# Output projection by seven block products, with its gated weights and block sums formed on GpSimd during the attention

## The chip, the cores and the metric

The kernel runs on one core of a Trainium2 chip. The metric is the device time in microseconds of one execution. The engines are called TensorE (PE; PEld is its weight load), VectorE (DVE), ScalarE (ACT), GpSimd (POOL) and SyncE (SP), which issues most of the DMAs.

## The reference, cut to what matters

One transformer layer over 1024 latent tokens of width 1024, with 256 context tokens. Two groups of heads (four retention heads, four heads of differential attention) give 1024 columns side by side; one output projection `w_out` follows, its result is gated by `g1` and added to `x`; then norm, MLP, norm.

```python
y_ret_lat = jax.nn.silu(rg_l) * ret_lat                    # 4 heads x 128 columns
y_diff_lat = diff_subln(diff_attention(dq_l, k_all, v_all, lam), subln_g, lambda_init)   # 4 x 128
out_lat = jnp.concatenate([y_ret_lat, y_diff_lat], axis=-1) @ w_out      # (1024, 1024)
x = x + g1 * out_lat
h = rms_norm(x, norm2_g) * (1.0 + sc2) + sh2               # into the MLP
```

All of it is in float32. A matmul is made in three passes: both operands are split in a high part (`F32R`, rounded) and a low part (the rest), and high x high, high x low and low x high are summed in PSUM (`passes`).

## The kernel before, in words

The stages come one after the other: modulation and input projection, retention (its results go to `yr_d` in DRAM, already split), differential attention, output projection, MLP.

The attention runs over 32 units (`Unit`, four heads times eight tiles of 128 queries). A unit has two score matrices of 128 x 1280 (`scores`, L897), their least values on VectorE (`least`, L900), two exponentials on ScalarE (`exp`, L904), the ratio of the two sums and the combination of the two on VectorE (`ratio`, L908 and L909; `combine`, L912, 128 x 1280 with both operands in SBUF), transposes and the product with the values (L917, L929), and a norm: a copy and a square on ScalarE (L933, L938), `e` on GpSimd (L940), `rstd` with L943 on VectorE and a power on GpSimd (L944), `norm` on ScalarE (L947), a transpose (L952), and the high and low part of the result (L955 on ScalarE, L958 on VectorE). The units overlap; the table `TAU` gives each step its place, and `in_order` fixes this order on PE, DVE, ACT and SP. What stands in `tc.issue_after(units[u].pool_ins.ins)` is issued behind L944 of unit `u`.

The output projection takes each of two column halves of `w_out` and in it eight row tiles of 128 tokens: 8 blocks times 3 passes of 128 x 512 matmuls into one bank, then a multiplication with `g1` and an addition to `x1` on VectorE. The weights of the first half are split in eight units in the middle of the attention, one block a unit: a cast on ScalarE (L1110), the low part on GpSimd (L1111). `yT` holds both parts of all activations in SBUF.

When a row tile of `x1` is complete, `norm2` stores it, squares it on ScalarE and scales it by a power made on GpSimd (L117). The first four rows are turned (`turned0`) beside the second half of the projection, the last four (`turned1`) beside the first products of the MLP. The MLP itself already uses seven block products; its first weights (`pre`, `raws`, in the slots `wra` and `wrb` of the pool `wst`) are loaded around the end of the attention, and `sums_in_place` adds blocks of them on GpSimd.

Of the kernel before, what the change touches and what calls it, by code (L numbers as in the profile page):

```python
# [26 lines left out]
H = 4  # L27
# [33 lines left out]
TAIL = 2  # L61
SPARE = (16, 4)
# [12 lines left out]
def kernel(  # L75
# [39 lines left out]
    def rsqrt(out_ap, in_ap, mul, eps, n):  # L115
        nc.vector.tensor_scalar(out=out_ap, in0=in_ap, scalar1=mul, scalar2=eps, op0=ALU.mult, op1=ALU.add)
        nc.gpsimd.tensor_tensor(out=out_ap, in0=out_ap, in1=mhalf[:, :n], op=ALU.pow)  # L117
# [29 lines left out]
    yr_d = [dr.tile([P, 2, H, 512], F32, name=f"yrd{i}") for i in range(2)]  # L147
# [7 lines left out]
    with ExitStack() as p1:  # L155
# [98 lines left out]
        class Step:  # L254
# [54 lines left out]
            def turn(self):  # L309
                pt = pst.tile([P, P], F32, name="pyt", tag="tr")  # L310
                nc.tensor.transpose(pt, self.y, ident)
                c = self.t % 2 * P
                if c == 0:
                    steps["out"] = rt.tile([P, 2, 2 * P], F32R, name="yr")
# [3 lines left out]
                if c == P:  # L318
                    o = (self.t % 4 - 1) * P
                    nc.sync.dma_start(out=yr_d[self.t // 4][:, :, self.h, o : o + 2 * P], in_=r32(steps["out"]))  # L320
# [562 lines left out]
        class Unit:  # L883
# [18 lines left out]
            def exp(self, m):  # L902
                self.p[m] = al.tile([P, LK], F32, name=f"p{m}")
                nc.scalar.activation(self.p[m], self.pa[m][:, :LK], AF.Exp, scale=-1.0, bias=self.mt[:, m : m + 1], accum_out=self.s[:, m : m + 1])  # L904
# [44 lines left out]
            def final(self):  # L949
                self.hi, self.lo = (yT[a][self.qt // 4][:, H + self.h, self.qt % 4 * P : (self.qt % 4 + 1) * P] for a in range(2))  # L950
# [3 lines left out]
            def high(self):  # L954
                nc.scalar.activation(self.hi, self.py, AF.Copy, scale=self.gain)  # L955

            def low(self):
                nc.vector.scalar_tensor_tensor(out=self.lo, in0=self.py, scalar=self.gain, in1=r32(self.hi), op0=ALU.mult, op1=ALU.subtract)  # L958
# [129 lines left out]
    ctx_ya = ctx.enter_context(ExitStack())  # L1088
    ypa = ctx_ya.enter_context(tc.tile_pool(name="ypa", bufs=1, reuse_waits="tile"))
    ctx_y = ctx.enter_context(ExitStack())  # L1090
    ypb = ctx_y.enter_context(tc.tile_pool(name="ypb", bufs=1, reuse_waits="tile"))
    yT = [[p.tile([P, KD, 512], F32R, name=f"yT{a}{i}") for i, p in enumerate((ypa, ypb))] for a in range(2)]

    ctx_wo = ctx.enter_context(ExitStack())
    wo = ctx_wo.enter_context(tc.tile_pool(name="wo", bufs=1, reuse_waits="tile"))

    g1 = wo.tile([P, D], F32, name="g1")

    def out_weights(n, sl, eng=nc.sync, low=nc.vector, lag=0):
        raws = []  # L1100
        for k in range(KD + lag):
            if k < KD:
                raw = wo.tile([P, 512], F32, name="woraw", bufs=4)
                eng.dma_start(out=raw, in_=w_out[n][:, k, :])
                raws.append(raw)
            yield
            if k >= lag:
                whi = wo.tile([P, 512], F32R, name="wohi", bufs=9)
                wlo = wo.tile([P, 512], F32R, name="wolo", bufs=9)
                nc.scalar.copy(whi, raws[k - lag])  # L1110
                low.tensor_tensor(out=wlo, in0=raws[k - lag], in1=r32(whi), op=ALU.subtract)  # L1111
                sl.append((whi, wlo))

    wo_first = []
    wo_gen = out_weights(0, wo_first, nc.gpsimd, nc.gpsimd, 2)


    with ExitStack() as p2:
        gap = p2.enter_context(tc.tile_pool(name="gap", bufs=1, reuse_waits="tile")).tile([P, 3200], F32, name="gap")
# [5 lines left out]
        for n in range(n_units + 8):  # L1125
# [3 lines left out]
            if n == 9:  # L1129
                with tc.issue_after(units[n - 5].pool_ins.ins):  # L1130
                    nc.gpsimd.dma_start(out=g1, in_=g1_d)
            if n in (8, 10, 12, 14):
                a, i = divmod(n // 2 - 4, 2)
# [705 lines left out]
```

## Time and profile before

| | us |
|---|---|
| median of 3 runs (lowest, highest) | 1388.02 (1388.01, 1388.24) |
| span of the profiled execution, first to last instruction | 1386.3 |
| own time of the profiled execution | not given apart from its span |
| attention, from its steady state to its last score tiles | 489.8 to 640.7 |
| end of the attention, output projection | 640.7 to 743.8 |

The granted TensorE clock was 0.999 in the mean. Positions are microseconds from the start of the span. In the rows of a profile, a line `L912 DVE ... out<-in x9 | 14.0, 1551 | 0.3` is a group of nine instructions of line 912 on VectorE, 14.0 us busy together, 1551 ns each in the mean, with 0.3 us of idle time ahead of them. In a row of the timeline the first two numbers are start and duration in us, and the brackets hold how long the engine had been idle and for whom it waited. Matmuls overlap: their rows show 0.39 us, but the next starts earlier, and the distance of starts counts.

### The profile page before, as it was taken

How to read it: one execution, taken by the hardware profiler on the slowest of the kernel's cores; microseconds unless marked ns; L12 is line 12 of the kernel's file. 1: busy time of each engine (PE TensorE's matmuls, PEld its weight loads, DVE VectorE, ACT ScalarE, POOL GpSimd, SP SyncE). 2: the span in 40 equal slices, each digit the busy share in tenths (PEclk: the TensorE clock that was granted, in tenths of full speed). 3: DMA queues.
4: the chain of work that ended last, by engine and by line, in shares of the span. 5: the costliest groups of instructions: out<-in, count | busy, mean ns of one | idle time of the engine just before them, and what ended most of it. 6: DMA issues, size and time to landing. Idle time of an engine off the chain costs nothing.

```text
span 1386.3 us, 19666 instructions
## 1 busy us (share of the span) xinstructions
PE 1365.4 (98%) x7028; PEld 1145.9 (83%) x7028; DVE 1018.0 (73%) x1512; ACT 738.6 (53%) x1410; POOL 346.4 (25%) x384
## 2 busy tenths in 40 slices
PE   8999999999999999999999999999999999999997
PEld 6788788888888799998888888888888888888886
DVE  5967866623467898896347998887778877898756
ACT  5536534313466789987037654555545555455533
POOL 1310001501446433411101343222332220043003
PEclk9999999999999999999999999999999999999999
DMA  9467887786678488631221223332323326953334
GB/s 384 153 206 252 295 265 249 254 273 185 191 221 231 133 217 186 140 94 70 106 99 46 92 107 114 114 114 92 114 100 113 111 69 224 393 180 109 122 99 152
DMA packets 107305, 231.14 MB, mean 167 GB/s; under 512 B 9604, under 2 KB 42884, under 8 KB 105288
## 3 DMA queue, kind: packets, MB, share of 16 engines
q1 hardware_dynamic: 98936, 204.73, 43.3%
q0 software_dynamic: 8128, 24.91, 7.9%
q8 instruction: 55, 0.90, 0.3%
q14 instruction: 42, 0.34, 0.1%
q10 hardware_dynamic: 144, 0.26, 0.1%
HBM read 165.37 MB, written 64.23 MB: 166 GB/s over the span
## 4 chain that ended last, share of the span: by engine, by line
PE 65%; DVE 1%; POOL 1%; issue 0%; ACT 0%; DMA 0%; SPq 0%; POOLq 0%; ACTq 0%; DVEq 0%
PE chain L131 6%; PE chain L132 6%; PE chain L133 6%; PE c L132 5%; PE c L133 5%; PE c L131 5%; PE pv L929 5%; PE pA L897 5%; PE third L131 3%; PE third L133 3%; PE third L132 3%; PE pt L917 2%; PE po L133 2%; PE po L132 2%; PE po L131 2%; PE second L131 1%
## 5 line engine op out<-in xcount | busy, mean ns | idle before, releaser
L131 PE MATMUL pl<-hT,whi 128*128 128x512 f32 x256 | 107.6, 420 | 0.0
L131 PE MATMUL chain<-T,whi 128*128 128x512 f32 x264 | 102.8, 389 | 0.0
L132 PE MATMUL chain<-T,whi 128*128 128x512 f32 x264 | 102.7, 389 | 0.0
L133 PE MATMUL chain<-T,wlo 128*128 128x512 f32 x264 | 102.7, 389 | 0.0
L133 PE MATMUL pl<-hT,wlo 128*128 128x512 f32 x256 | 100.4, 392 | 0.0
L132 PE MATMUL pl<-hT,whi 128*128 128x512 f32 x256 | 100.3, 392 | 0.0
L900 DVE TENSOR_REDUCE mt<-pA 128x1 f32<-128x1280 f32 x64 | 95.2, 1490 | 3.8 <-PE pA L897 2.3
L133 PE MATMUL c<-whi,ghl 128*128 128x512 f32 x232 | 90.4, 390 | 0.0
L131 PE MATMUL c<-whi,ghl 128*128 128x512 f32 x232 | 90.3, 389 | 0.0
L132 PE MATMUL c<-wlo,ghl 128*128 128x512 f32 x232 | 90.3, 389 | 0.0
L1310 POOL TENSOR_TENSOR cmb<-wrb 128x512 f32<-128x512 f32 x20 | 30.3, 1517 | 237.6 <-DMA wrb<-w_up 157.3
L897 PE MATMUL pA<-ks,qhl 128*128 128x512 f32 (+1 forms) x384 | 89.6, 368 | 0.0
L904 ACT ACTIVATE p<-pA,mt 128x1280 f32<-128x1280 f32 x64 | 85.5, 1336 | 3.8 <-DVE mt L900 3.4
L131 PE MATMUL pn<-whi,hT 128*128 128x512 f32 x192 | 85.0, 443 | 0.0
L445 ACT ACTIVATE xb<-pl 32x512 f32<-32x512 f32 (+1 forms) x88 | 52.0, 591 | 61.6 <-PE pl L133 41.9
L1161 ACT CAST whi<-cmb 128x512 fp32r<-128x512 f32 x62 | 38.4, 622 | 77.5 <-PE chain L132 64.3
L929 PE MATMUL pv<-va,aT 128*128 128x128 f32 x640 | 77.1, 276 | 0.4 <-DVE yT L958 0.3
L897 PEld LDWEIGHTS pA<-ks,qhl 128*128 128x128 f32 x384 | 67.9, 189 | 11.5
L133 PE MATMUL pn<-whi,hT 128*128 128x512 f32 x192 | 75.8, 396 | 1.0 <-POOL hT L610 1.0
L132 PE MATMUL pn<-wlo,hT 128*128 128x512 f32 x192 | 75.4, 393 | 0.0
L929 PEld LDWEIGHTS pv<-va,aT 128*128 128x128 f32 x640 | 74.0, 192 | 1.2 <-DVE yT L958 0.8
L1162 DVE TENSOR_TENSOR wlo<-cmb,whi 128x512 fp32r<-128x512 f32 x62 | 58.7, 951 | 18.1 <-ACT whi L1161 18.1
(336 smaller groups left out, 3889.7 us busy)
## 6 DMA issues: line engine op xcount, KB each, us to landing
raw<-w_in SPq DMA_DIRECT2D x32, 512.0 KB, 6.0
wm<-w_mod SPq DMA_DIRECT2D x32, 512.0 KB, 4.6
wra<-w_up SPq DMA_DIRECT2D x24, 512.0 KB, 3.3
wrb<-w_up SPq DMA_DIRECT2D x23, 512.0 KB, 3.5
W<-w_down SPq DMA_DIRECT2D x44, 256.0 KB, 6.2
ad<-s SPq DMA_DIRECT2D x20, 512.0 KB, 3.4
wra<-ad SPq DMA_DIRECT2D x20, 512.0 KB, 3.3
wrb<-ad SPq DMA_DIRECT2D x18, 512.0 KB, 4.6
```

The source lines that it names most:

```text
L131: mm(ps, lh, rh, start=first, stop=False, skip_group_check=more)
L132: mm(ps, lh, rl, start=False, stop=False, skip_group_check=more)
L133: mm(ps, ll, rh, start=False, stop=last, skip_group_check=more)
L445: nc.scalar.activation(xb[q * blk : (q + 1) * blk, :], pt[o : o + blk, :], AF.Copy, scale=scale)
L897: mm(self.pa[m][:, c0:c1], self.q[:, i, m, qs], self.k[:, m, c0:c1], start=(i == 0), stop=(i == 1))
L900: nc.vector.tensor_reduce(out=self.mt[:, m : m + 1], in_=self.pa[m][:, :LK], axis=AX.X, op=ALU.min)
L904: nc.scalar.activation(self.p[m], self.pa[m][:, :LK], AF.Exp, scale=-1.0, bias=self.mt[:, m : m + 1], accum_out=self.s[:, m : m + 1])
L917: nc.tensor.transpose(self.pt[g][:, i, :], self.p[0][:, (4 * g + i) * P : (4 * g + i + 1) * P], ident)
L929: mm(self.pv, self.aT[:, c, :], self.v[:, c, :], start=(c == 0), stop=(c == NKT - 1))
L1161: nc.scalar.copy(hi, src)
L1162: nc.vector.tensor_tensor(out=lo, in0=src, in1=r32(hi), op=ALU.subtract)
L1310: nc.gpsimd.tensor_tensor(out=s1, in0=b1, in1=b2, op=ALU.add)
```

## The change

The activations Y and the weights W are seen as 2 x 2 blocks (tokens 0 to 511 and 512 to 1023; retention and attention columns; the two halves of the outputs), and the product is made by seven block products with sums of blocks (the variant of Winograd) in place of eight. A block product is four row tiles times four blocks of 128 times three passes, 48 matmuls. Four of the seven products go into one set of four banks (`chain`, `oc`), which is added to `x1` after each of them and never started anew; the others go into a second set (`os`, `of`).

The gate is multiplied into the weights. A generator `weight_blocks` yields GpSimd operations of 128 x 512: the gated blocks with their high and low parts, and the differences t1 to t4, which go to DRAM (`wt_d`) through the SP queue and come back in the projection. It also forms `s3` from the retention results, and a list `later` holds sums that need finished heads of the attention. `next_op` gives one such operation, and three are issued behind L944 (now L953) of each unit from iteration 6 on, until the 76 are used up. The loads of `w_out` and `g1` move from GpSimd's queue to SP's. In a unit L958 (the low part on VectorE) is gone; results stay whole in `y12` and `y22` and are split in the projection, or per head for `opb`.

On GpSimd, in a stretch of the attention, this stood before (L944 is the power, L940 `e`, L1111 a low part of a projection weight, L981 a load of queries):

```order
178 L944 TENSOR_TENSOR ssa<-ssa,mhalf 128x1
179 L940 TENSOR_TENSOR e<-sa 128x1
180 L1111 TENSOR_TENSOR wolo<-woraw,wohi 128x512
181 L944 TENSOR_TENSOR ssa<-ssa,mhalf 128x1
182 L940 TENSOR_TENSOR e<-sa 128x1
183 L981 DMA qhl<-dq_89 64x4x512
184 L1111 TENSOR_TENSOR wolo<-woraw,wohi 128x512
```

and this stands there now (L953 is the power, L949 `e`, L1140 an operation of `weight_blocks`, L1192 one of `later`, L997 the load of queries):

```order
206 L953 TENSOR_TENSOR ssa<-ssa,mhalf 128x1
207 L1140 TENSOR_TENSOR w11o<-w_5629,w11o 128x512
208 L1140 TENSOR_TENSOR w21o<-w_5631,g_5016 128x512
209 L949 TENSOR_TENSOR e<-sa 128x1
210 L997 DMA qhl<-dq_89 64x4x512
211 L1140 TENSOR_TENSOR w_5631<-w_5631,g_5016 128x512
212 L997 DMA qhl<-dq_89 64x4x512
213 L953 TENSOR_TENSOR ssa<-ssa,mhalf 128x1
```

Where one operation of 128 x 512 (or none) stood between two powers, there are three, and the loads of queries, keys and values stand between them.

At the end of the projection GpSimd had this before (L117 is the power for a row tile of `x1`, L1225 to L1227 are `sums_in_place`, L1307 is a sum of the MLP's weights; `x7` stands for seven in a row):

```order
221 L1225 TENSOR_TENSOR wrb<-wrb 128x512
222 L1226 TENSOR_TENSOR wra<-wrb,wra 128x512
223 L1227 TENSOR_TENSOR wra<-wra 128x512
224 L117 TENSOR_TENSOR sm_7022<-sm_7022,mhalf 128x1 x7
225 L1307 TENSOR_TENSOR cmb<-wrb,wra 128x512
```

and has this now (L118, L1299 to L1301, L1455):

```order
276 L118 TENSOR_TENSOR sm_7088<-sm_7088,mhalf 128x1 x4
277 L1299 TENSOR_TENSOR wrb<-wrb 128x512
278 L1300 TENSOR_TENSOR wra<-wrb,wra 128x512
279 L1301 TENSOR_TENSOR wra<-wra 128x512
280 L118 TENSOR_TENSOR sm_7088<-sm_7088,mhalf 128x1 x3
281 L1455 TENSOR_TENSOR cmb<-wrb,wra 128x512
282 L118 TENSOR_TENSOR sm_7088<-sm_7088,mhalf 128x1
```

The sums stood ahead of all but one of these powers; now four powers come first, and the powers of the last four rows stand behind sums that wait for loads into `wra` and `wrb`.

On SP the first loads of `w_up` stood ahead of and right behind the loads of `x1`; now they stand behind the stores of the first four rows of `x1`, since `s2o` and `s3o` lie in their slots.

The diff, cut to its core:

```diff
             def turn(self):
...
+                if self.t >= 4:
+                    if c == 0:
+                        steps["out"] = rt.tile([P, 2, 2 * P], F32, name="yrf", tag="yr")
+                    nc.scalar.copy(steps["out"][:, 0, c : c + P], pt)
+                    if c == P:
+                        nc.sync.dma_start(out=yr_d[1][:, self.h, o : o + 2 * P], in_=steps["out"][:, 0, :])
+                    return
...
             def high(self):
-                nc.scalar.activation(self.hi, self.py, AF.Copy, scale=self.gain)
+                nc.scalar.activation(self.y, self.py, AF.Copy, scale=self.gain)
             def low(self):
-                nc.vector.scalar_tensor_tensor(out=self.lo, in0=self.py, scalar=self.gain, in1=r32(self.hi), op0=ALU.mult, op1=ALU.subtract)
+                if self.qt == 3:
+                    opb[self.h] = op_tile("b", self.h)
+                    nc.scalar.copy(opb[self.h][:, 0, :], yraw("y12", self.h))
+                    later.append(dict(out=opb[self.h][:, 1, :], in0=yraw("y12", self.h), in1=r32(opb[self.h][:, 0, :]), op=ALU.subtract))
+                if self.qt == 7:
+                    s2, y22, y12 = (yraw(n, self.h) for n in ("s2", "y22", "y12"))
+                    later.append(dict(out=s2, in0=y22, in1=yraw("s3", self.h), op=ALU.subtract))
+                    later.append(dict(out=y12, in0=y12, in1=s2, op=ALU.subtract))
...
-    wo_first = []
-    wo_gen = out_weights(0, wo_first, nc.gpsimd, nc.gpsimd, 2)
+    def weight_blocks():
+        g1 = opp.tile([P, D], F32, name="g1", tag="r1")
+        nc.sync.dma_start(out=g1, in_=g1_d)
...
+        def split(o, raw, a, b, f):
+            op(o[:, 0, :], a, b, f)
+            yield
+            op(raw, a, b, f)
+            yield
+            op(o[:, 1, :], raw, r32(o[:, 0, :]), ALU.subtract)
+            yield
+        def kept(n, c, o, a, b):
+            op(o, a, b, ALU.subtract)
+            nc.sync.dma_start(out=wt_d[n][c], in_=o)
+        load(0, "w11", "w21", "w12", "w22")
+        for c in range(4):
+            if c < 3:
+                load(c + 1, "w11", "w21", "w12")
...
+            yield from split(u_ops[c], w11, w11, ga, ALU.mult)
+            yield from split(v_ops[c], w21, w21, ga, ALU.mult)
+            if c == 0:
+                for k in range(4):
+                    a_ops[k] = op_tile("a", k, "y11o")
+                    nc.gpsimd.dma_start(out=a_ops[k], in_=yr_d[0][:, k])
...
+            op(w12, w12, gb, ALU.mult)
+            yield
+            yield from split(w_ops[c], w22, w22, gb, ALU.mult)
+            kept("t1", c, w11, w12, w11)
+            yield
+            kept("t3", c, w12, w22, w12)
+            yield
+            kept("t2", c, w22, w22, w11)
+            yield
+            kept("t4", c, w21, w21, w22)
...
+            if c == 0:
+                for k in range(4):
+                    for a in range(2):
+                        s3, part = yraw("s3", k), r32(a_ops[k][:, a, :])
+                        op(s3, *((part, s3, ALU.subtract) if a == 0 else (s3, part, ALU.add)))
+                        yield
+    def next_op():
+        if later and len(raw_tiles) > 3:
+            nc.gpsimd.tensor_tensor(**later.pop(0))
+        else:
+            next(prep, None)
...
-                if op == "f" and n >= 12:
-                    next(wo_gen, None)
+                if op == "f" and 6 <= n < n_units + 4:
+                    with tc.issue_after(units[u].pool_ins.ins):
+                        for _ in range(3):
+                            next_op()
...
+        def out_product(ps, r, y, w, first):
+            rs = slice(r * P, (r + 1) * P)
+            for k in range(4):
+                passes(ps, (y[k][:, 0, rs], y[k][:, 1, rs]), (w[k][:, 0, :], w[k][:, 1, :]), first and k == 0, k == 3, not first)
+                tick()
+        def to_x1(t, cols, ps):
+            nc.vector.tensor_tensor(out=x1[t][:, cols], in0=ps, in1=x1[t][:, cols], op=ALU.add)
+        def split_into(o, src):
+            nc.scalar.copy(o[:, 0, :], src)
+            nc.vector.tensor_tensor(out=o[:, 1, :], in0=src, in1=r32(o[:, 0, :]), op=ALU.subtract)
+        def c_ops(n):
+            o = [wst.tile([P, 2, C], F32R, name=n, tag=("wra", "wrb")[k % 2]) for k in range(4)]
+            for k in range(4):
+                split_into(o[k], yraw(n, k))
+            return o
...
+        for r in range(4):
+            out_product(chain[r], r, a_ops, u_ops, True)
+            to_x1(r, left, chain[r])
...
+        with tc.issue_after(units[n_units - 1].exp_ins):
+            s2o = c_ops("s2")
+        t2o = split_all("u", "t2o", t2raw)
+        with tc.issue_after(units[n_units - 1].pool_ins.ins):
+            for k in range(4):
+                for a in range(2):
+                    nc.gpsimd.tensor_tensor(out=yraw("s2", k), in0=yraw("s2", k), in1=r32(a_ops[k][:, a, :]), op=ALU.add)
...
+        for r in range(4):
+            out_product(other[r], r, opb, v_ops, True)
+            to_x1(r, left, other[r])
+        t1o = split_all("v", "t1o", t1raw)
+        s1o = split_all("a", "s1o", [yraw("s2", k) for k in range(4)])
+        for r in range(4):
+            out_product(chain[r], r, s2o, t2o, False)
+            to_x1(r, right, chain[r])
...
+        for r in range(4):
+            out_product(other[r], r, s1o, t1o, True)
+            to_x1(4 + r, right, other[r])
...
+        for r in range(4):
+            out_product(other[r], r, s4o, w_ops, False)
+            to_x1(r, right, other[r])
+            norm2(r)
...
+        beside(turned0(), 0.5, -3.0)
+        for r in range(4):
+            out_product(chain[r], r, s3o, t3o, False)
+            to_x1(4 + r, right, chain[r])
+        pre = [raw_load("wra" if j < 2 else "wrb", w_up[j]) for j in range(NPRE)]
+        early = [[split_op(a[:, c : c + 4, :]) for c in (0, 4)] for a in pre]
+        raws = [up_load(j) for j in range(NSUM)]
+        sums_in_place(*raws[0])
+        for r in (3, 0, 1, 2):
+            out_product(chain[r], r, y22o, t4o, False)
+            to_x1(4 + r, left, chain[r])
+            scaled = norm2(4 + r)
+        with tc.issue_after(scaled):
+            sums_in_place(*raws[1])
...
-    beside(turned1(), 0.36, 0.0)
+    beside(turned1(), 0.4, -1.2)
```

More of the change, by code (lines that the diff above doesn't have):

```diff
@@ L1097 @@
[L1097 to L1105, printed above, removed]
-            yield
[L1107 to L1112, printed above, removed]
@@ L1172, in product @@
         for k in range(4):
[L1173 removed]
+            passes(ps, (hi[:, k, :], lo[:, k, :]), (tt[k][:, 0, :], tt[k][:, 1, :]), first and k == 0, k == 3, not first)
             tick()
[L1176 removed]
     rawp = ExitStack()
```

150 lines of the change are left out of this document (91 added, 59 removed).

## The prediction

> **What bounds the kernel now.** I read the stages around the output projection first, then one unit of the attention instruction by instruction, and last the places where GpSimd and VectorE work at the same time.
>
> The stages, in us (busy time of PE, PEld, DVE, ACT, POOL): the last third of the attention, then its end, the rest of the projection, and the start of the MLP.
>
> ```profile
> 589.20:640.73 51.53, 51.53 (x385) 48.42 (x386) 46.76 (x63) 46.15 (x108) 9.00 (x22) 1.00 0.25 68
> 640.73:657.10 16.37, 15.21 (x109) 12.66 (x108) 6.31 (x13) 10.16 (x29) 2.52 (x6) 1.00 0.31 110
> 657.10:743.80 86.70, 86.70 (x398) 71.80 (x399) 42.22 (x68) 24.12 (x40) 10.58 (x12) 1.00 0.26 98
> 743.80:800.00 56.20, 56.20 (x264) 46.12 (x263) 52.65 (x70) 37.64 (x63) 18.31 (x11) 1.00 0.19 66
> ```
>
> PE is busy throughout, so removed matmuls are worth their full time where nothing else comes up. But in the attention VectorE and ScalarE are at about 90% as well, with GpSimd at 9.00 of 51.53 where it has no projection weights to work on. That is the gap into which the change puts its work. In the start of the MLP VectorE is at 52.65 of 56.20.
>
> One unit of the attention in its steady state, from the square-root step of one unit to that of the next:
>
> ```profile
> 634.74 0.16 DVE L943 SCALAR_TENSOR_TENSOR ssa<-e,ssa 128x1 f32<-128x1 f32 x1 [0.27 <-ACT jka L938]
> 634.98 0.55 POOL L944 TENSOR_TENSOR ssa<-ssa,mhalf 128x1 f32<-128x1 f32 x1 [5.04 <-DVE ssa L943]
> ...
> 635.49 0.19 POOL L940 TENSOR_TENSOR e<-sa 128x1 f32<-128x1 f32 x1
> ...
> 636.22 0.40 ACT L947 ACTIVATE oa<-oa,ssa 128x128 f32<-128x128 f32 x1
> ...
> 636.45 0.34 DVE L958 SCALAR_TENSOR_TENSOR yT<-pty,subg,yT 128x128 fp32r<-128x128 f32 x1
> ...
> 638.41 0.22 DVE L909 SCALAR_TENSOR_TENSOR r<-r,sa,nlam 128x1 f32<-128x1 f32 x1
> 638.67 1.55 DVE L912 SCALAR_TENSOR_TENSOR p<-p,r,p 128x1280 f32<-128x1280 f32 x1
> ...
> 640.49 0.16 DVE L943 SCALAR_TENSOR_TENSOR ssa<-e,ssa 128x1 f32<-128x1 f32 x1 [0.27 <-ACT jka L938]
> 640.73 0.55 POOL L944 TENSOR_TENSOR ssa<-ssa,mhalf 128x1 f32<-128x1 f32 x1 [5.04 <-DVE ssa L943]
> ```
>
> A unit takes 5.75 us (640.73 - 634.98). GpSimd does L944 and L940 and then waits 5.04 us for the next L943. VectorE's work in nine such units:
>
> ```profile
> L900 DVE TENSOR_REDUCE mt<-pA 128x1 f32<-128x1280 f32 x18 | 26.8, 1491 | 1.2 <-PE pA L897 0.8
> L912 DVE SCALAR_TENSOR_TENSOR p<-p,r,p 128x1280 f32<-128x1280 f32 x9 | 14.0, 1551 | 0.3
> L958 DVE SCALAR_TENSOR_TENSOR yT<-pty,subg,yT 128x128 fp32r<-128x128 f32 x9 | 3.1, 342 | 0.0
> L909 DVE SCALAR_TENSOR_TENSOR r<-r,sa,nlam 128x1 f32<-128x1 f32 x9 | 2.2, 239 | 0.9
> L943 DVE SCALAR_TENSOR_TENSOR ssa<-e,ssa 128x1 f32<-128x1 f32 x9 | 1.4, 160 | 2.2 <-ACT jka L938 2.2
> L908 DVE RECIPROCAL r<-sa 128x1 f32<-128x1 f32 x9 | 1.4, 153 | 0.0
> ```
>
> These are 48.9 us, 5.43 a unit. The change takes L958 out (0.34), so VectorE has 5.09 us of work in 5.75 and can lose about 0.66 us a unit before it, and not PE, sets the pace.
>
> **The matmuls.** Before, 16 tiles times 8 blocks times 3 passes are 384 matmuls; after, 7 products times 4 row tiles times 4 blocks times 3 passes are 336. Their price is the distance of their starts, 51 matmuls between these two rows:
>
> ```profile
> 674.05 0.39 PE L131 MATMUL po<-wohi,yT 128*128 128x512 f32 x1
> ...
> 685.61 0.39 PE L131 MATMUL po<-wohi,yT 128*128 128x512 f32 x1
> ```
>
> 11.56 us / 51 = 0.227 us. 48 fewer are **-10.9 us**, all on the path while PE stays fed.
>
> **Feeding PE in the projection.** The gate multiply goes, and instead VectorE adds each of 28 banks to x1 and splits 36 operands together with ScalarE.
>
> ```profile
> L1242 DVE TENSOR_TENSOR gated<-po,g 128x512 f32<-128x512 f32 x16 | 11.0, 690 | 26.2 <-PE po L133 26.2
> L1243 DVE TENSOR_TENSOR x<-gated,x 128x512 f32<-128x512 f32 x16 | 12.2, 762 | 0.9 <-DMA x<-x 0.5
> L1110 ACT CAST wohi<-woraw 128x512 fp32r<-128x512 f32 x16 | 9.9, 623 | 34.8 <-PE po L133 32.6 <-DMA woraw<-w_out 2.0
> ```
>
> VectorE: 28 + 36 operations of 0.69 are 44.2 us, in place of 23.2 us here and eight splits (5.5 us). That adds 15.5 to the 42.22 of a stage that shrinks to about 76 us, so it fits; ScalarE gets 20 more casts of 0.62, 12.5 us on 24.12. One product is 48 x 0.227 = 10.9 us of PE, and eight splits for the next cost 5.5 us of VectorE. The tightest is the third product: ScalarE's casts for s1o stand ahead of those for t2o and wait for GpSimd's sums, at most seven of them after the last unit, about 1.3 us each plus 0.5 where VectorE gets in between, 12.6 us; with 2.5 us of casts and one split that is some 15.5 us. PE then still has about 85 matmuls of the first two products, 19.3 us, so 4 us are left. I cost this at 0; without that cover PE would wait the difference, some microseconds once.
>
> **The end of the projection.** The slots wra and wrb hold projection operands up to the sixth product, so the first w_up loads come after it and not during the attention's end. GpSimd now has sums_in_place ahead of the powers of x1's last rows, and the turns of those rows wait behind them. From here on the prices are these:
>
> ```profile
> 670.20 1.29 POOL L1225 TENSOR_TENSOR wrb<-wrb 128x512 f32<-128x512 f32 x1
> ...
> 671.57 1.62 POOL L1226 TENSOR_TENSOR wra<-wrb,wra 128x512 f32<-128x512 f32 x1
> ```
>
> Three sums and a fourth operation for the MLP, 1.3 to 1.6 us each, stand in the seventh product's 10.9 us plus the 18 matmuls (4.1 us) ahead of the first turn, in which the loads must land too. It nearly fits. Bounds: 0, and the four operations in full (6 us); a gain is excluded, as PE is full there. As VectorE has 3.5 us to spare in the 56.2 that follow, I take a value nearer the lower end, **+1.5 us**.
>
> **GpSimd beside the attention.** 76 operations of 128x512 are spread over 24 units, three behind each L944. Where such work has met the attention before, at its start (last queries rotated on GpSimd), the rows are these:
>
> ```profile
> 472.64 1.26 POOL L1054 TENSOR_TENSOR xa<-xa,rtab 128x512 f32<-128x512 f32 x1 [16.13 <-DMA xb<-xa]
> ...
> 473.88 1.26 POOL L1054 TENSOR_TENSOR xb<-xb,rtab 128x512 f32<-128x512 f32 x1
> 473.90 1.25 DVE L909 SCALAR_TENSOR_TENSOR r<-r,sa,nlam 128x1 f32<-128x1 f32 x1
> ...
> 475.19 2.67 DVE L912 SCALAR_TENSOR_TENSOR p<-p,r,p 128x1280 f32<-128x1280 f32 x1
> 475.21 1.29 POOL L1054 TENSOR_TENSOR xhl<-xa,xb 128x512 fp32r<-128x512 f32 x1
> ...
> 477.94 0.16 DVE L943 SCALAR_TENSOR_TENSOR ssa<-e,ssa 128x1 f32<-128x1 f32 x1
> ...
> 481.07 1.43 DVE L909 SCALAR_TENSOR_TENSOR r<-r,sa,nlam 128x1 f32<-128x1 f32 x1
> 481.17 1.30 POOL L1054 TENSOR_TENSOR xhl<-xa,xhl 128x512 fp32r<-128x512 f32 x1
> ...
> 484.00 0.15 DVE L943 SCALAR_TENSOR_TENSOR ssa<-e,ssa 128x1 f32<-128x1 f32 x1
> ```
>
> L909, 0.22 us alone, lasts exactly to the end of the GpSimd operation beside it (1.25 and 1.43). Between L909 and L912 the next GpSimd operation slips in, and L912 takes 2.67 instead of 1.55: it starts in earnest when that ends (476.50) and needs 1.36 from there. [...]
>
> Now three operations a unit. Counted from L943: L944 from 0.24 to 0.79, then operations at 1.24 us (473.88 - 472.64) each, with L940 (0.19) between them: up to 2.0, 3.3 and 4.6 to 4.7. L909 comes at 3.67 with PE in front (638.41 - 634.74), at 3.13 with VectorE behind (481.07 - 477.94). Either way it meets the second or third operation; L912 starts at about 4.6 and is done 1.36 to 1.55 later, and L943 follows at 6.0 to 6.3. So the unit goes from 5.75 to about 6.2 us, and VectorE, not PE, sets it. The unit from 477.94 to 484.00, with two operations in it, took 6.06.
>
> The bounds: 5.75, if the operations fall where VectorE has only its L900; and 6.8, if GpSimd's DMA issues, hidden so far in its 5 us of waiting, come on top:
>
> ```profile
> L981 POOL DMA_DIRECT2D qhl<-dq x10 | 6.9, 700 | 0.0
> L986 POOL DMA_DIRECT2D ks<-dk x4 | 2.5, 630 | 0.0
> L989 POOL DMA_DIRECT2D va<-dvd x2 | 2.0, 1017 | 0.0
> ```
>
> Eight units issue 4, 2 and 1 of them, 5.1 us, 0.63 a unit; they delay L944, for which ScalarE's norm (L947) and behind it the next exponential wait. I take 6.2, the value of the walk through one unit: 24 x 0.45 = **+10.8 us**.
>
> [...]
>
> **What goes away.** Eight units so far carry one split of projection weights each, with a cast of 0.62 us on ScalarE:
>
> ```profile
> 541.50 0.55 POOL L944 TENSOR_TENSOR ssa<-ssa,mhalf 128x1 f32<-128x1 f32 x1 [4.88 <-DVE ssa L943]
> ...
> 589.20 0.55 POOL L944 TENSOR_TENSOR ssa<-ssa,mhalf 128x1 f32<-128x1 f32 x1 [3.20 <-DVE ssa L943]
> ```
>
> 47.70 us are 5.96 a unit, 0.21 above 5.75: **-1.7 us**. The new casts for opb are four in 32 units and cost nothing beside that. The loads of w_out go from GpSimd's queue to SP's, which in the attention carries nothing else; their stores and reads of the block sums add 8 MB where the DMA engines are busy 0.25 to 0.31: 0. In the retention 16 half-tiles lose their low part on VectorE: 0, as PE is full there.
>
> **The sum:** -10.9 + 1.5 + 10.8 - 1.7 = -0.3 us. Against the profiled execution's span of 1386.3 this is 1386.0; the runs' median of 1388.02 stands 1.7 above that span, so 1387.7. What a measurement of this kernel can tell from no change is 0.2%, 2.8 us.
>
> **The rivals.**
> *The unit stays near 5.8.* If L944 runs late by about 1.2 us, the third operation falls behind L912 and only L909's wait is left, 0.3 to 0.6 us, which VectorE's 0.66 us covers. For it speaks that L947 has 0.69 us of slack (636.22 against L944's end at 635.53); against it that any unit whose L940 stands early loses the pattern again. Then 24 x 0.05 = 1.2: 1378, up to 1384 when half the units keep it.
> *GpSimd becomes the bound* (the other side). Three operations, L944, L940 and a blocked L912 are already 5.9 us; the DMA issues make it 6.5 in their units. The change saves 11.1 us beside this term, so from 6.33 us a unit on (24 x 0.58 = 13.9) it is slower by more than 0.2%. At 6.6: 24 x 0.85 = 20.4, so 1397.
> *The projection starves.* If a product's operands come late each time by 1 to 2 us, or the turns wait for the sums in full, 5 to 10 us are lost: 1393 to 1398. Against it speaks the spare time of VectorE and ScalarE there.
>
> **How the numbers follow.** The forecast (units of 6.05 to 6.35 us, 1384 to 1391) gets 0.35, the units near 5.8 get 0.33, GpSimd as the bound 0.27, a starving projection 0.05. Faster is the second case and 0.05 of the first, 0.38; same 0.24; slower the rest, 0.38. The range 1378 to 1399 leaves out the last of the two outer cases; the likeliest case by itself spans 1384 to 1391.
>
> **What would show it.** Right: units 6.0 to 6.3 us apart by L944, L909 and L912 stretched in most of the 24 units, PE with gaps there and none in the projection, and the projection 10 to 11 us shorter. Wrong: PE full in the attention (then 1378), L944 starting over 1 us behind L943 with ScalarE waiting for it (then over 1391), or PE gaps at the third product or at the turns of x1's last rows.

## The result, and the profile after

The changed kernel takes 1398.03 us (median of 4 runs, 1396.24 to 1401.37) against 1388.13 of the kernel before on the same chips: a ratio of 1.0073, 95% interval 1.0059 to 1.0087. It is 0.7% slower. The profiled execution took 1397.08 us with a span of 1395.3, which is 9.0 more than before.

Both traces cut at the same places: 24 units of the attention (from the third L953, before L944, to the 27th), from there to the MLP's first product, to the first matmul of `third`, to the first product of the down projection, to the end. Columns: stretch and its length, then busy time and number of instructions of PE, PEld, DVE, ACT and POOL, the granted clock, the DMA share and GB/s. After:

```profile
489.56:642.82 153.26, 147.86 (x1034) 131.83 (x1035) 141.73 (x145) 127.75 (x292) 128.03 (x142) 0.99 0.60 144
642.82:746.00 103.18, 101.99 (x540) 85.69 (x539) 72.70 (x109) 58.67 (x120) 28.94 (x30) 1.00 0.40 147
746.00:776.07 30.07, 26.53 (x130) 20.92 (x128) 27.49 (x43) 22.15 (x39) 9.77 (x8) 1.00 0.12 49
776.07:1169.95 393.88, 392.31 (x1730) 324.27 (x1728) 326.50 (x366) 202.96 (x295) 120.51 (x81) 1.00 0.30 106
1169.95:1395.30 225.35, 215.69 (x949) 177.52 (x947) 172.00 (x237) 106.49 (x172) 40.27 (x29) 0.99 0.53 187
```

Before:

```profile
489.76:629.23 139.47, 139.43 (x1034) 129.88 (x1033) 124.64 (x169) 127.28 (x297) 47.13 (x88) 1.00 0.66 150
629.23:743.80 114.57, 113.41 (x592) 95.28 (x591) 58.93 (x95) 44.54 (x92) 14.52 (x22) 1.00 0.24 90
743.80:769.54 25.74, 25.74 (x130) 20.93 (x129) 23.55 (x38) 20.27 (x36) 3.40 (x3) 1.00 0.05 21
769.54:1162.29 392.75, 392.00 (x1730) 324.23 (x1728) 327.43 (x367) 203.08 (x296) 119.69 (x81) 1.00 0.30 106
1162.29:1386.30 224.01, 215.77 (x949) 177.51 (x947) 172.01 (x237) 106.26 (x172) 39.75 (x29) 0.99 0.53 188
```

The attention lost 13.8 us with the same 1034 matmuls in it; the projection gained 11.4 (540 matmuls for 592); the start of the MLP lost 4.3, and the rest of the program 2.5. Less the 0.2 us by which the 24 units begin earlier, these are the 9.0.

In the attention the combination and the ratio on VectorE are longer, the least values are not. After (L921 and L918), then before (L912 and L909), over the 24 units:

```profile
L909 DVE TENSOR_REDUCE mt<-pA 128x1 f32<-128x1280 f32 x49 | 70.8, 1480 | 0.6 <-PE pA L906 0.6
L921 DVE SCALAR_TENSOR_TENSOR p<-p,r,p 128x1280 f32<-128x1280 f32 x24 | 57.4, 2391 | 0.8
L918 DVE SCALAR_TENSOR_TENSOR r<-r,sa,nlam 128x1 f32<-128x1 f32 x24 | 12.4, 515 | 6.3 <-ACT p L913 4.2
```

```profile
L900 DVE TENSOR_REDUCE mt<-pA 128x1 f32<-128x1280 f32 x48 | 71.5, 1490 | 2.4 <-PE pA L897 1.5
L912 DVE SCALAR_TENSOR_TENSOR p<-p,r,p 128x1280 f32<-128x1280 f32 x24 | 37.2, 1552 | 0.8
...
L909 DVE SCALAR_TENSOR_TENSOR r<-r,sa,nlam 128x1 f32<-128x1 f32 x24 | 5.4, 227 | 2.7 <-ACT p L904 0.7
```

But the loss is not spread evenly. A quiet unit, and behind it one with two DMA issues on GpSimd, from L953 to L953 (rows of VectorE and GpSimd):

```profile
550.52 0.55 POOL L953 TENSOR_TENSOR ssa<-ssa,mhalf 128x1 f32<-128x1 f32 x1 [1.50 <-DVE ssa L952]
...
553.41 0.22 DVE L918 SCALAR_TENSOR_TENSOR r<-r,sa,nlam 128x1 f32<-128x1 f32 x1
...
553.65 1.29 POOL L1140 TENSOR_TENSOR w<-w,g 128x512 f32<-128x512 f32 x1
...
553.67 2.62 DVE L921 SCALAR_TENSOR_TENSOR p<-p,r,p 128x1280 f32<-128x1280 f32 x1
...
556.43 0.55 POOL L953 TENSOR_TENSOR ssa<-ssa,mhalf 128x1 f32<-128x1 f32 x1 [1.50 <-DVE ssa L952]
...
561.97 0.15 DVE L952 SCALAR_TENSOR_TENSOR ssa<-e,ssa 128x1 f32<-128x1 f32 x1
...
562.04 1.40 POOL L997 DMA_DIRECT2D qhl<-dq  x2
563.36 0.66 POOL L953 TENSOR_TENSOR ssa<-ssa,mhalf 128x1 f32<-128x1 f32 x1
```

The quiet unit takes 5.91 us: the third GpSimd operation starts 0.02 us ahead of L921 and makes it 2.62 us. The other takes 6.93: L952 is done at 562.12, but the two issues stand ahead of the power on GpSimd. Over the 24 units, nine (eight with DMA issues, and the first) together lie 11.9 us above nine times 5.75, the other fifteen 3.4 above theirs. The first alone took 8.93:

```profile
493.74 1.91 POOL L1140 TENSOR_TENSOR w11o<-w,g 128x512 fp32r<-128x512 f32 x1 [3.61 <-DMA w<-w_out]
```

Its weights landed 3.6 us after GpSimd was ready for them, and L949 and the next power stood behind.

Behind the attention PE waits at these places (total, times, longest, in us); before, only `third` (0.7) and the one at the end of the attention were there:

```profile
PE pt L1275 <- DVE x L1269: 1.8, 2, 1.5
PE third L132 <- DVE ub L1581: 1.6, 1, 1.6
PE fifth L132 <- ACT T L1282: 1.2, 1, 1.2
PE c L134 <- DVE ghl L1745: 1.1, 1, 1.1
...
PE fifth L133 <- DVE T L1283: 0.5, 1, 0.5
```

All but one lie in the first 87 us of the MLP, where VectorE is nearly full (27.49 of the first 30.07 us). The last row of `x1` on its way to PE:

```profile
751.02 1.35 POOL L1299 TENSOR_TENSOR wrb<-wrb 128x512 f32<-128x512 f32 x1
751.16 1.75 DVE L1269 TENSOR_SCALAR x<-x,sm 128x1024 f32<-128x1024 f32 x1
...
752.97 0.44 PE L1275 MATMUL pt<-ident,x 128*128 128x128 f32 x2 [1.48 <-DVE x L1269]
```

Its scaling, 0.74 us alone, takes 1.75 beside a sum of `sums_in_place`.

### The profile page after: what moved, and what is told of

Its sections match the earlier page's. It is cut to its first block, busy times and chain, and to the rows that moved or that the text cites. A ratio compares the mean times of both kernels' runs of the same rounds, so it can differ in the third digit from the quotient of the medians.

```text
span 1395.3 us, 19708 instructions
## 1 busy us (share of the span) xinstructions
PE 1363.2 (98%) x6980; PEld 1138.7 (82%) x6980; DVE 1049.6 (75%) x1488; ACT 755.5 (54%) x1434; POOL 450.7 (32%) x451
## 4 chain that ended last, share of the span: by engine, by line
PE 51%; DVE 6%; POOL 5%; DMA 4%; issue 3%; ACT 2%; SPq 0%; POOLq 0%; DVEq 0%; ACTq 0%
PE chain L133 5%; PE chain L134 5%; PE chain L132 5%; PE c L134 4%; PE c L133 4%; PE c L132 4%; PE third L132 3%; PE third L134 3%; PE third L133 3%; DMA W<-w_down 2%; POOL w L1140 1%; PE pA L906 1%; PE pv L938 1%; PE second L134 1%; PE second L133 1%
## 5 line engine op out<-in xcount | busy, mean ns | idle before, releaser
L909 DVE TENSOR_REDUCE mt<-pA 128x1 f32<-128x1280 f32 x64 | 92.8, 1481 | 2.4 <-PE pA L906 2.1
L1237 ACT CAST whi<-wra 128x512 fp32r<-128x512 f32 x55 | 34.0, 623 | 70.1 <-PE third L133 43.5
```

Source lines behind the costliest of these rows:

```text
L909: nc.vector.tensor_reduce(out=self.mt[:, m : m + 1], in_=self.pa[m][:, :LK], axis=AX.X, op=ALU.min)
L1237: nc.scalar.copy(hi, src)
```

## The experiments

Theory I for the attention: GpSimd's DMA issues, which it could hide in 5 us of waiting before, come on top of its operations, and the rest is the first wait. Theory W, nearer to the prediction: every unit pays for the time that GpSimd's operations hold VectorE (2.39 us a combination for 1.55). For the start of the MLP, Q: the powers wait behind the sums; L: all that hangs on the late loads of `w_up` crowds VectorE and GpSimd there. Ratios are to the kernel before, with 95% intervals; the stretches are those above, each from one profiled execution.

| run | us | ratio | 24 units | to the MLP | to `third` |
|---|---|---|---|---|---|
| changed | 1398.03 | 1.0073 (1.0059, 1.0087) | 153.26 | 103.18 | 30.07 |
| e1 one block formed | 1392.96 | 1.0027 (1.0016, 1.0038) | 146.15 | 103.66 | 31.24 |
| e2 issues on SyncE | 1388.92 | 1.0005 (0.9996, 1.0014) | 144.75 | 103.24 | 30.11 |
| e3 two units later | 1398.30 | 1.0069 (1.0057, 1.0082) | 151.18 | 105.36 | 30.62 |
| e4 sums last | 1400.14 | 1.0082 (1.0068, 1.0096) | 152.66 | 103.11 | 33.41 |
| e5 e2, one unit later | 1388.62 | 1.0003 (0.9995, 1.0012) | 142.86 | 103.27 | 31.05 |
| e6 e5, turns as before | 1389.10 | 1.0004 (0.9995, 1.0014) | 142.23 | 103.27 | 31.05 |
| e7 no wait for store | 1399.52 | 1.0081 (1.0068, 1.0094) | 154.04 | 103.18 | 31.34 |
| e8 e6, second load late | 1388.90 | 1.0001 (0.9993, 1.0010) | 143.04 | 103.29 | 32.01 |
| e9 own slots | 1400.83 | 1.0096 (1.0082, 1.0109) | 153.14 | 110.43 | 26.48 |
| e10 e5 and e9 | 1390.20 | 1.0018 (1.0009, 1.0027) | 142.45 | 109.94 | 26.47 |
| e11 e10, turns as before | 1389.96 | 1.0017 (1.0008, 1.0027) | 142.53 | 111.13 | 26.60 |
| e12 e10, sums between | 1388.06 | 0.9997 (0.9988, 1.0006) | 142.83 | 106.19 | 26.45 |
| e13 e12, turns as before | 1387.09 | 0.9993 (0.9984, 1.0002) | 143.18 | 109.83 | 26.60 |
| e14 before, 3 operations more | 1422.32 | 1.0241 (1.0227, 1.0256) | 170.34 | 115.58 | 25.73 |
| e15 e12, first turns later | 1384.76 | 0.9972 (0.9964, 0.9981) | 142.38 | 103.27 | 27.07 |
| e16 e15, last turns later | 1382.49 | 0.9958 (0.9945, 0.9972) | 143.24 | 103.24 | 26.89 |

### The attention: e1, e2, e3, e14, e5

**e1.** Only the first of four blocks of weights is formed; the other three reuse it, which changes values.

```diff
+            if c > 0:
+                u_ops[c], v_ops[c], w_ops[c] = u_ops[0], v_ops[0], w_ops[0]
...
+                continue
```

> Left out: the gated weights and their sums are formed for the first of four blocks of rows only; the other three blocks reuse the first block's operands, and for the sums the raw weights are stored as loaded. Matmuls, loads and GpSimd's DMA issues stay. Theory W (the work itself: GpSimd operations and VectorE exclude each other, each unit with three operations pays about 0.45 us): the units without work go back to 5.75 us, also those with DMA issues; 42 of 76 operations gone, 14 units times 0.45 = 6.3 us less than the changed kernel, 1391 to 1392. Theory I (most of the loss is DMA issues on GpSimd and the first wait for the weights, operations alone cost about 0.2 us a unit): the same units at 5.75 too where GpSimd's issues are hidden again by its waiting, since the sum of the two is what counts; the first ten units stay as slow as they are (6.8 to 8.9 us where issues or the wait stand), and the gain is 14 times 0.2 plus the excess of the issuing units behind them, 3 + 3 = 6 us. Both give about 1392; what tells them apart here is only whether a unit with issues and no operations stands at 5.75 (the issues cost only together with operations) or above.

Measured 1392.96. A unit in e1 with three issues and two operations:

```profile
583.87 0.56 POOL L953 TENSOR_TENSOR ssa<-ssa,mhalf 128x1 f32<-128x1 f32 x1 [3.78 <-DVE ssa L952]
584.41 1.27 POOL L1199 TENSOR_TENSOR s<-y,s 128x512 f32<-128x512 f32 x1
585.65 0.67 POOL L997 DMA_DIRECT2D qhl<-dq  x1
586.33 1.29 POOL L1199 TENSOR_TENSOR y<-y,s 128x512 f32<-128x512 f32 x1
587.55 0.62 POOL L1002 DMA_DIRECT2D ks<-dk  x1
588.16 1.00 POOL L1005 DMA_DIRECT2D va<-dvd  x1
589.63 0.56 POOL L953 TENSOR_TENSOR ssa<-ssa,mhalf 128x1 f32<-128x1 f32 x1 [0.48 <-DVE ssa L952]
```

It takes 5.76 us, with 0.48 of GpSimd's time left: three issues fit beside two operations. Two units with two issues and no operation took 6.31 and 6.36, but GpSimd stood idle for 4.3 us in each, and the units behind them took 5.50 and 5.51; the fourteen units from 554.83 on are at 5.80 in the mean, as before (5.81 over the 24). So issues alone fit into a unit; three operations and the issues, in the changed kernel, did not (6.45 to 8.2).

**e2.** The loads of the attention and of `y11o` are issued by SyncE.

```diff
+            q, view = (nc.sync, r32) if i >= 12 else (nc.gpsimd, lambda ap: ap)
...
-                        nc.gpsimd.dma_start(out=cur["q"][a * 64 : (a + 1) * 64], in_=dq_d[h]...
+                        q.dma_start(out=view(cur["q"][a * 64 : (a + 1) * 64]), in_=dq_d[h]...
...
-                    nc.gpsimd.dma_start(out=a_ops[k], in_=yr_d[0][:, k])
+                    nc.sync.dma_start(out=r32(a_ops[k]), in_=yr_d[0][:, k])
```

> From the 13th unit on the loads of queries, keys and values are issued by SyncE instead of GpSimd, and so are the four loads of y11o. Theory I: the units that stood at 6.4 to 8.2 us fall to the 5.9 to 6.1 of the others; their excess over 6.0 adds up to about 7 us, so 1390 to 1392. Theory W: VectorE sets the unit by the three operations whoever issues the loads, 1396 to 1398.

Measured 1388.92, 9.1 less than the changed kernel and 1.1 below theory I's range, and 8.5 less in the 24 units. All units but the first are now at 5.76 to 6.16 us, while VectorE's combination is as slow as it was:

```profile
L921 DVE SCALAR_TENSOR_TENSOR p<-p,r,p 128x1280 f32<-128x1280 f32 x24 | 58.5, 2437 | 0.8
```

Theory I stands: VectorE is held as long as in the changed kernel (2.44 us a combination for 2.39), and 9.1 of the 9.9 us of loss are gone. An issue of queries takes GpSimd 0.70 us before and after the change, and what the rows of the changed kernel show is this time ahead of the power in its full queue.

**e3.** The operations start two units later, the first loads do not. (This leaves the first head's `s2` to be formed from an `s3` that is not complete, which changes values and no work.)

> The loads of the first block stay where they are, the operations on GpSimd start two units later. If the wait of 3.6 us for the first weights sits on the path: the first unit goes from 8.9 to about 5.8 us, two units run without operations, and the six operations come at the attention's end where GpSimd waits anyway: 3 us less than the changed kernel, 1394 to 1396. If VectorE's time by operation alone counts: no change, 1397 to 1399.

Measured 1398.30, no gain. The first unit fell from 8.93 to 5.50 as expected, but other units met the loads at another place, or got a fourth operation, and five of them took 7.33 to 8.21. In such a unit of e3 VectorE's 0.22 us L918 is held for 2.31:

```profile
517.70 1.29 POOL L1140 TENSOR_TENSOR w<-w,g 128x512 f32<-128x512 f32 x1
...
517.94 2.31 DVE L918 SCALAR_TENSOR_TENSOR r<-r,sa,nlam 128x1 f32<-128x1 f32 x1
518.94 1.29 POOL L1193 TENSOR_TENSOR opb<-y,opb 128x512 fp32r<-128x512 f32 x1
```

**e14.** The kernel before, with three multiplications a unit whose results nothing reads.

```diff
+        nc.gpsimd.memset(gap[:, 512:1536], 0.5)
...
+                if op == "f" and 6 <= n < n_units + 4:
+                    with tc.issue_after(units[u].pool_ins.ins):
+                        for i in range(3):
+                            nc.gpsimd.tensor_tensor(out=gap[:, 0:512], in0=gap[:, 512:1024], in1=gap[:, 1024:1536], op=ALU.mult)
```

> The kernel before, with three multiplications of 128x512 on GpSimd behind the square-root step of every unit from the seventh on; they work on a buffer of constants that nothing else reads (added work, no other change). If GpSimd's operations and VectorE's exclude each other at the price that the changed kernel's quiet units show (5.9 to 6.05 us), the units without loads go from 5.75 to 6.0 to 6.3 (the operation that the change removed from VectorE, 0.34 us, is still there), the units with loads or weights to 6.5 to 7: 24 units 8 to 15 us longer, 1396 to 1403. If the dependences of the weights (loads, stores, slots) and not the operations were the cost: less than 3 us, 1388 to 1391.

Measured 1422.32: the 24 units took 30.9 us more, twice the upper end of what I expected. The last quiet units are at 6.01 to 6.03, as expected; most units with loads or the weights' own operation took 7.2 to 8.2, not 6.5 to 7. So operations that depend on nothing make such a loss by themselves, as soon as a fourth operation or issues come to the three. Its size is not the changed kernel's: the eight units that also carry L1111, which the change removes, lie 16.6 us above 5.75, and L958 is still there.

**e5.** e2, started one unit later.

> The loads issued by SyncE as in e2, and the operations on GpSimd start one unit later than in the change, so that the first weights have landed. If the clash with the DMA issues was what gave back the gain of e3: the first unit falls from 8.9 to about 5.8 us, all others stay at 5.8 to 6.0, and the sum is 3 us less than e2, 1385 to 1386.5. If the three operations by themselves meet VectorE worse when they start from another place: units of 6.2 and more, 1388 to 1390.

The first unit fell to 5.51 and the 24 units by 1.9 us (the next two took 6.29 and 6.65, the second with a wait of PE of 1.3 us for keys; the unit behind the 24 took 6.03 for 5.51). The total stayed where e2 was, 1388.62. PE came earlier to the MLP and took 0.9 us longer up to `third`; the rest is not explained, and both kernels vary by over 4 us from run to run.

### From the projection to the MLP: e4, e6 to e13, e15, e16

**e4.** The first `sums_in_place` stands behind all powers.

> The first three sums of w_up stand behind the powers of all rows of x1 on GpSimd, not ahead of the last four. Theory Q (the powers wait behind the sums, and the turns of x1 behind the powers): the two waits of PE for x (1.8 us) go, and what follows from them (1.7 us at the fifth product), 1394.5 to 1396.5. Theory L (VectorE is full there since the first loads of w_up come 65 us later than before, and their splits with them): the waits move, total within 1 us of the changed kernel, 1397 to 1399.

Measured 1400.14, 2.1 us above the changed kernel and outside both ranges: the powers were early, but PE's wait for x grew from 1.8 to 3.8 us, since the last scaling now stood behind a split of `w_up` on VectorE that waited 1.8 us for its cast, and then again took 1.75 us beside the sums. Q alone falls.

**e7.** The changed kernel, without the wait for that store.

```diff
-        nc.sync.dma_start(out=x1_d[t], in_=x1[t])
+        nc.sync.dma_start(out=x1_d[t], in_=x1[t] if t < 4 else x[t * P : (t + 1) * P, :])
```

> The changed kernel, but for rows 4 to 7 of x1 the store before the scaling takes x from DRAM instead of x1 (left out: these rows' projection in the residual that the end of the kernel adds), so the scaling in place has no store to wait for. If the store of the last row, issued behind the loads of w_up, is what holds the scaling: PE's waits for x go from 1.8 to below 0.5 us, 1396 to 1397. If GpSimd's sums hold VectorE: the waits stay, 1397.5 to 1399.

Measured 1399.52, 0.5 above the second range, the waits for x at 3.2 us: the store by itself was not the cause either.

**e6 and e8** kept e5 and moved the last turns, or the second load.

> As e5, with the turns of x1's last rows set beside the first products of the MLP by the rate and the due time of the kernel before (0.36 and 0.0 in place of 0.4 and -1.2). If the changed kernel asks for the rows too early: PE's waits for x (1.8 us) go and nothing else comes, 1383.5 to 1385. If VectorE is behind there whatever the order (the splits of the early w_up loads now stand at this place): PE waits as long a few products later, within 1 us of e5.

> As e6, with the second pair of w_up blocks for the sums loaded after the stores of x1's last rows instead of ahead of them. If the transfers ahead hold the stores: 0.5 to 1.5 us less than e6. If not: the sums of the second pair come later, the fifth product waits for their split, 0 to 2 us more than e6.

Neither gained: 1389.10 and 1388.90. In e6 I had the direction wrong: 0.36 and 0.0 bring the first turn after three blocks, the change's 0.4 and -1.2 after six. PE waited 1.9 us at the first turn there, and then its clock was halved (below).

**e9, e10, e11.** `s3o` and `y22o` move to slots that are free in time, so that `wra` and `wrb` are free after the third product; loads, sums and splits of `w_up` come earlier.

```diff
-        s3o = c_ops("s3")
+        s3o = split_all("a", "s3o", [yraw("s3", k) for k in range(4)])
...
-        y22o = split_all("a", "y22o", [yraw("y22", k) for k in range(4)])
+        y22o = split_all("b", "y22o", [yraw("y22", k) for k in range(4)])
```

> The changed kernel, with s3o formed in the slots of s1o and y22o in those of opb, so that the slots wra and wrb are free after the third product: the loads of w_up start some 30 us earlier, both sums_in_place follow on GpSimd before the powers, and the early splits stand among the sixth product's work. Theory L (the late loads of w_up crowd VectorE, GpSimd and the stores at the start of the MLP): PE's waits for x, for the fifth and the third product (1.8 + 1.7 + 0.8 us) go, 3 to 5 us less than the changed kernel, 1393 to 1396. Rival (VectorE is full there by the work of the MLP's own operands): the waits move by a product or two, less than 1.5 us, 1396.5 to 1399.

> e9 and e5 together. If their gains add: e5's 1386 to 1389 less 3 to 5 us, and less the 1.7 us by which the clock at half rate after PE's wait at the start of the MLP had cost e5: 1381 to 1385, faster than before by 3 to 7 us. If PE, coming sooner from the attention, outruns the operands of the third or sixth product: gaps there, 1386 to 1389.

> e10 with the turns of x1's last rows by the rate and due time of before. With the splits out of the way it should make little difference, 1380 to 1385; if the due time of -1.2 is what makes PE wait for x, it is 1 to 3 us less than e10.

The start of the MLP is repaired (26.5 us for 30.1), as theory L says, but the totals, 1400.83, 1390.20 and 1389.96, lie above all the ranges: 7 to 8 us are lost in the projection. In e10 the second sums wait for their load (the row names a store, but the load into `wrb` landed at 715.07, later), with the power of the fourth row behind them:

```profile
715.19 1.26 POOL L1303 TENSOR_TENSOR wrb<-wrb 128x512 f32<-128x512 f32 x1 [3.08 <-DMA x1d<-x]
...
718.21 0.54 POOL L118 TENSOR_TENSOR sm<-sm,mhalf 128x1 f32<-128x1 f32 x1
...
718.79 1.75 DVE L1273 TENSOR_SCALAR x<-x,sm 128x1024 f32<-128x1024 f32 x1 [1.66 <-POOL sm L118]
...
720.59 0.48 PE L1279 MATMUL pt<-ident,x 128*128 128x128 f32 x1 [3.08 <-DVE x L1273]
```

**e12, e13** put these sums between the powers of the first and of the last four rows.

> As e10, with the second sums_in_place between the powers of rows 0 to 3 and those of rows 4 to 7. In e10 it stood ahead of the fourth power and PE waited 5.5 us for x there, and ran at half clock for some 3.4 us behind it. If that order was the whole loss: these waits fall below 1 us, 5 to 7 us less than e10, 1383 to 1385.5. If the loads of w_up hold the stores of x1 in any case: half the wait stays, 1386 to 1389.

> As e12, with the turns of x1's last rows by the rate and due time of before. Within 1 us of e12 if the early splits have made room; otherwise 1 to 2 us less, 1382 to 1385.

1388.06 and 1387.09, within the error of before and in the second range of e12's two; 3.1 and 3.9 us of waits for x were left, of 5.5 in e10.

**e15, e16.** Both sets of turns come later.

```diff
-        beside(turned0(), 0.5, -3.0)
+        beside(turned0(), 0.5, -6.0)
...
-    beside(turned1(), 0.4, -1.2)
+    beside(turned1(), 0.5, -3.0)
```

> As e12, with the turns of x1's first four rows begun after 14 blocks of the last two products in place of 8 (due -6.0 for -3.0). PE's waits of 3.1 us for x in the sixth product go if VectorE and GpSimd only needed the time: 2.5 to 4 us less than e12, 1384 to 1385.5, faster than before. If VectorE is the bound from there to the first sums of the MLP: the time moves to the waits of the third products, 1387 to 1389.

> As e15, with the turns of the last four rows begun after 8 blocks in place of 6 and then faster (0.5, -3.0). 0 to 1 us less than e15 if PE waits for x at the start of the MLP; 1 to 2 us more if T1 to T4 come too late for the fifth product.

1384.76, as forecast, and 1382.49, 2.3 us less than e15 where 0 to 1 was forecast: e16 beats both kernels, 0.42% faster than before (interval 0.28 to 0.55%). In the two profiles, one execution each, e16's gain over e15 does not stand at the start of the MLP (26.89 for 27.07) but behind it: 2.0 us from `third` to the down projection, where a wait of PE of 0.9 us is gone and another fell from 1.6 to 0.8. Against before, the projection keeps 11.3 us, the attention gives 3.8 of them back, the MLP's start 1.2, and the down projection 1.1 (a wait for `ghl`, in every version of the change; its cause was not found). Of the attention's 3.8 us, 1.5 stand in one unit of 7.28 us, in which PE waits 1.95 us for keys (`ks`) whose loads landed 14.6 to 17.3 us after their issue (9.8 to 12.2 in the kernel before); no run tried to move them. In the MLP's start VectorE is at 24.79 us of 26.89 there, against 27.49 of 30.07 in the changed kernel:

```profile
735.98:762.87 26.89, 26.20 (x129) 20.99 (x128) 24.79 (x41) 22.10 (x40) 4.11 (x4) 1.00 0.10 40
```

## Why the prediction was wrong

The forecast was 1387.7, no change; it came out 10.3 higher, 1 us from the rival "GpSimd becomes the bound" (1397). That closeness is partly luck: the rival's sum has 20.4 us for 24 units of 6.6, the units showed 15.3 above 5.75, and the difference came from the start of the MLP and behind it.

- **Matmuls, -10.9:** right. The stretch with them became 11.4 us shorter.
- **Feeding the projection, 0:** right. PE was busy in all 76.44 us from 669.56 to 746.00.
- **GpSimd beside the attention, +10.8 less 1.7:** this step failed. 9.1 us were forecast and 13.8 measured. The walk through one quiet unit was taken for all 24, with VectorE setting the pace. Its value, 6.2, was too high for the quiet ones (5.98 in the mean of fifteen): it met the combination as it happened (2.39 us for 1.55), the ratio less often than forecast (0.52 us in the mean, for 1.25 or 1.43). What the sum left out were GpSimd's DMA issues, which I had counted (0.63 us a unit, without the four loads of `y11o`, 2.3 us) and used only for the upper end. The eight units with issues lay 8.7 us above 5.75, and e2, which moved the issues alone, took back 8.5. The sign I had named, a power over 1 us behind its step on VectorE, stood in the first unit (2.5) and in three with issues (1.1 to 1.25).
- **The first weights:** not priced at all; 3.2 us, the first unit's excess. In e5, where it was gone, the units behind it grew, and 1.9 us of it were kept in the 24. I had taken the DMA engines as 0.25 to 0.31 busy, which holds from 589 us on; over the 24 units they were at 0.66 already before.
- **End of the projection, +1.5 (0 to 6):** measured 4.3, and 1.1 more up to the end of the third products' wait; with PE's waits for x, the other sign I had named. This term was too small as well. I priced GpSimd's queue alone. What also moved with the loads were the splits on VectorE, in a stretch where I had counted 3.5 us of spare time, and the sums that held VectorE's scaling (1.75 us for 0.74). In e9 the loads, sums and splits came early together and this stretch was repaired; which of the three counted most was not separated. e12 to e16 showed that order alone takes away what e9 lost in the projection.
- **The rivals:** the first did not come, as the quiet units stood at 5.98 and not near 5.8. The second had the right engine, but not "6.6" as a value for all units: 6.45 to 8.2 in the units with issues, and 5.98 in the others. The third did not come: the projection was fed, and the turns cost 1.8 us of PE's waits, not 5 to 10.

## What to carry to other kernels

Work for an engine that seems idle has to be fitted unit by unit, with the rare instructions of its queue (here DMA issues of 0.7 us) in the sum of the units that carry them, not averaged over all. An engine's idle share says nothing of the order: in a full stretch each instruction that moves with a slot moves the waits of all that stand behind it. And a saving of 11 us of matmuls became 5.8 us of time (e16 against before) only after waits elsewhere had been taken away one by one.

## What the runs showed of the hardware that was not expected

**Behind a wait of PE of 1.9 us its clock fell to half, though not behind every such wait; what this cost differed by stage.** In e6 PE was idle for 1.9 us within 736 to 739, and then ran at about half clock for 3.4 us; the column of interest is the third from the right:

```profile
736.00:737.00 1.00, 0.32 (x2) 0.00 (x0) 0.59 (x2) 0.58 (x1) 1.00 (x2) 1.00 0.45 180
737.00:738.00 1.00, 0.00 (x0) 0.00 (x0) 1.00 (x1) 0.57 (x2) 0.59 (x1) 1.00 0.88 365
738.00:739.00 1.00, 0.80 (x4) 0.44 (x5) 0.87 (x3) 0.00 (x0) 0.71 (x1) 1.00 0.43 172
739.00:740.00 1.00, 1.00 (x4) 0.80 (x5) 0.69 (x1) 0.92 (x2) 1.00 (x2) 0.61 0.00 0
740.00:741.00 1.00, 1.00 (x4) 0.81 (x3) 1.00 (x2) 0.23 (x1) 0.92 (x2) 0.50 0.00 0
741.00:742.00 1.00, 1.00 (x5) 0.68 (x4) 1.00 (x2) 0.00 (x0) 1.00 (x1) 0.50 0.00 0
742.00:743.00 1.00, 1.00 (x7) 0.82 (x7) 0.75 (x1) 0.78 (x1) 0.92 (x2) 0.68 0.00 0
```

The four last rows lack 1.7 us of full clock. The changed kernel shows the same behind its first unit's wait of 1.88 us: from 501.75 to 505.50 the clock was 0.54 in the mean, again 1.7 us less than full. In e10 the matmuls behind the wait of 3.08 us start 0.42 to 0.43 us apart from 721.29 to 723.42, against 0.22 to 0.23 ahead of its waits. The length of the wait alone did not decide: behind one of 1.95 us in e16 (ended at 503.25) the clock was 1.00, and at the start of the MLP 1.82 us of waits (0.34 and 1.48) left it at 1.00 in the changed kernel.

In the projection, where PE set the pace, the slow clock cost its full price: e10 took 6.7 us longer there than e5, the 5.0 us of its two waits (1.92 and 3.08) and 1.7 behind them. In the attention of the changed kernel, where VectorE was busy in all of the 3.75 us from 501.75 to 505.50, it cost nothing that can be seen: the unit behind the first took 6.01 us, and the fifteen quiet units, it among them, 5.98 in the mean. Whether it explains that some kernels vary more from run to run (e6: 1384.66 to 1392.48; e16: 1382.09 to 1382.81) is not shown: one execution of each was profiled, e6's was its fastest, and the kernel before, with no such wait in its profile, varied from 1385.98 to 1390.31 beside e16.

**GpSimd held VectorE for several operations in a row.** In e14 a VectorE instruction of 0.22 us lasted 4.09, over three GpSimd operations that followed each other without a gap:

```profile
563.72 4.09 DVE L909 SCALAR_TENSOR_TENSOR r<-r,sa,nlam 128x1 f32<-128x1 f32 x1
564.01 1.30 POOL L1144 TENSOR_TENSOR gap<-gap 128x512 f32<-128x512 f32 x1
...
565.25 1.30 POOL L1111 TENSOR_TENSOR wolo<-woraw,wohi 128x512 fp32r<-128x512 f32 x1
...
566.50 1.28 POOL L1144 TENSOR_TENSOR gap<-gap 128x512 f32<-128x512 f32 x1
```

I had expected VectorE to come next when the first of them ended; here it came after the third. Why it was not done in the 0.29 us ahead of the first of them is not shown.
